# Splitting normed rows for an expert gather during the projection ahead of it

## Chip, cores and metric

The kernel runs on one core of one Trainium2 chip. The metric is device microseconds of one execution of the whole kernel; lower is better.

## The reference

One decoder layer over 512 tokens of width 1024, all in float32. The change lies where the second part, a cross-attention, ends and the third, a mixture of experts, begins:

```python
h = layer_norm(ALPHA * h + o @ w_xo, ln2_g, ln2_b)      # o: attention over 256 memory tokens
g_logits = h @ w_router_group + b_router_group           # 8 groups, the best one is taken
e_logits = h @ w_router_expert + b_router_expert         # 8 experts in it, the best two are taken
...
hb = silu(xb @ w_gate[e]) * (xb @ w_up[e])               # xb: the tokens of expert e, hidden width 256
y_rows = hb @ w_down[e]
h = layer_norm(ALPHA * h + segment_sum(y_rows * weight), ln3_g, ln3_b)
```

Each of the 64 experts has a gate, an up and a down matrix of 1 MB.

## The kernel before

The 512 tokens are four blocks (t = 0 to 3) of 128 rows, one row to a partition. The tensor `h2` holds the rows after the cross-attention.

**Output projection.** `proj_tm` (L275) computes `o @ w_xo` in two column halves. Each matrix is split into a high and a low part, since the matmul of the fast type keeps only part of a float32: `A.copy` on ScalarE (ACT) rounds to the high part, a subtraction on VectorE (DVE) or GpSimd (POOL) gives the low one. While the second half runs block by block, the loop at L1073 puts the router between its matmuls: `rows_T(t)` transposes the rows on TensorE (PE) and copies them with ACT (L959), `route(t)` makes the logits and picks experts with short DVE operations, `norm(t)` writes the normed rows (without scale and bias) on ACT, and `finish(t)` counts with PE (`prk`) which slot each token takes at its expert and writes a one-hot tile `G0[t]` on DVE (L1046, L1047).

**First gather.** After the projection, `h2_split(t)` splits the normed rows into `h2h` (ACT, L1108) and `h2l` (POOL or DVE, L1111); the two big tiles take over memory that the projection's input held (`pool2a`). `gather0(t)` multiplies them with the one-hot tile, so that the tokens of the first 256 slots are gathered, transposed, in PSUM (`px0`); `to_XT` applies the norm's scale and bias there and writes `XTs[0]`. Independently POOL applies scale and bias to `h2` itself in 32 operations of 256 columns (L1145, L1146), since the experts' results are added to it later. The two row vectors `gbc2` and `bbc2` are loaded during the projection.

**Experts.** They come in 20 columns of 128 slots, some of two and some of four or five experts. `hidden_of(c)` multiplies with the gate matrices, then with the up matrices (`pu`), and makes `hb` with a SiLU on ACT and a product on DVE (L1180). `down` transposes `hb` (`ph`), copies it to `hT` on DVE (L1251), and multiplies with the down matrices (`pd`, L1256). `scaled` splits the result into `yh` (ACT) and `yl` (DVE), and `combine` adds it to `h2` by a one-hot matmul (`pc`, L1376) and a DVE sum (L1377). Columns 0 and 1 go first. During column 0 the experts are put in order of their counts (`ppos`, `ptb`); from that DVE works out `gslot`, every token's slot (L1302). `next_pair(1)` writes the one-hot tiles `G1` from it and gathers columns 2 and 3 (`px1`, L1235, L1236). Then come the down projections of columns 0 and 1, and `ptab`, a table of weights and tokens by slot (L1332).

**What orders the work.** From the projection to `ptab`, PE, POOL and the DMA queue of SyncE (SP) run in the order in which the code is written (`manual_schedule`). DVE and ACT run in an order that a scheduler fixed when the program was built, and so does PE from column 2 on. Every engine executes its list in order.

**Weights.** `WeightStream` loads expert matrices into a ring of ten slots of 1 MB (`NSLOT`): gates and ups of column 0, then of column 1, then the downs, then column by column. A load is issued once the matmuls that read the slot before are done. Eight slots open as soon as the attention's memory is free, the last two behind the projection.

Of the kernel before, what the change touches and what calls it, by code (L numbers as in the profile page):

```python
# [60 lines left out]
def tile_layer(ctx, tc, x, mem, positions, w_in, attn_sinks, conv_w, conv_b, b_igate, b_fgate, ml_norm_g,  # L61
# [680 lines left out]
    small = ctx.enter_context(tc.tile_pool(name="small", bufs=2, reuse_waits="tile"))  # L742
    pool2a = ctx.enter_context(tc.tile_pool(name="big2a", bufs=2, reuse_waits="tile"))
    stack2b = pa.enter_context(ExitStack())
# [134 lines left out]
    stack2b.close()  # L879
    open_slots(NSLOT - 2)  # L880
    stack2c = pa.enter_context(ExitStack())
# [41 lines left out]
    rT2 = [lnw.tile([P, NK, P], name=f"rT{i}") for i in range(2)]  # L923
    gbc2, bbc2 = lnw.tile([P, D], name="gbc2"), lnw.tile([P, D], name="bbc2")

# [18 lines left out]
    slot0 = keep.tile([P, NT, 2], F32, name="slot0")  # L944
    gslot = keep.tile([P, NT, 2], F32, name="gslot")
    E = keep.tile([P, NT, 2, NE], BF16, name="E")
    Es = keep.tile([P, NT, NE], BF16, name="Es")
    scr64 = work.tile([P, 1, NE], F32, name="scr64")

    def rows_T(t):  # L950

        r = h2[:, t, :]
        rT = rT2[t % 2]
        for c in range(2):
# [59 lines left out]
    def xo_consume(b, t, ps):  # L1014
        if b == 0:
            lns2[t] = LayerNorm(small, h2[:, t, :], gbc2, bbc2, f"2{t}")
# [7 lines left out]
    for i in range(4):  # L1024
        step(gen, 4)
        if i == 2:
            nc.sync.dma_start(gbc2, row(ln2_g).to_broadcast([P, D]))
            nc.sync.dma_start(bbc2, row(ln2_b).to_broadcast([P, D]))
        wstream.ahead(i)
# [39 lines left out]
    def finish(t):  # L1069
        ranks(t)  # L1070
        onehot_tile(G0, slot0, t)

    for t in range(NT):  # L1073
        if t > 0:
            step(gen, 1)
            rows_T(t - 1)
            if t > 1:
                finish(t - 2)
            step(gen, 1)
            lns2[t - 1].scales()  # L1080
            route(t - 1)
            norm(t - 1)
        else:
            step(gen, 1)
        step(gen, 1)
    run(gen)
    stack2c.close()
    open_slots(2)
    wstream.ahead(len(wslots))
    h2h = bigtile(pool2a, "h2h", F32R).rearrange("p (t n) -> p t n", t=NT)  # L1090
    h2l = bigtile(pool2a, "h2l", F32R).rearrange("p (t n) -> p t n", t=NT)

    h2hv = h2h.rearrange("s t (k p) -> s t k p", k=NK)
    h2lv = h2l.rearrange("s t (k p) -> s t k p", k=NK)
    h2v = h2.rearrange("s t (p k) -> s t k p", k=NK)
    px0 = [(psA if c < 3 else psB).tile([P, 2, 256], F32, name=f"px0{c}", tag="psA" if c < 3 else "psB") for c in range(4)]

    def gather0(t):

        for k in range(NK):  # L1100
# [5 lines left out]
    def h2_split(t, on):  # L1106

        A.copy(h2hv[:, t], h2v[:, t])  # L1108
        n = 4 if on is V else 2
        for k in range(0, NK, n):  # L1110
            on.tensor_tensor(h2lv[:, t, k:k + n, :], h2v[:, t, k:k + n, :], h2hv[:, t, k:k + n, :].bitcast(F32), ALU.subtract)  # L1111
            yield

    rows_T(3)
    lo = h2_split(0, G)
    step(lo, 2)
    lns2[3].scales()
    run(lo)
    route(3)
    finish(2)  # L1120
    gather0(0)
    run(h2_split(1, G))
    norm(3)
    gather0(1)
    run(h2_split(2, V))
    finish(3)
    gather0(2)
    run(h2_split(3, V))
    gather0(3)
# [11 lines left out]
    for c in range(4):  # L1141
        to_XT(XTs[0], px0[c], c)
    for t in range(NT):
        for o in range(0, D, 256):
            G.tensor_tensor(h2[:, t, o:o + 256], h2[:, t, o:o + 256], gbc2[:, o:o + 256], ALU.mult)  # L1145
            G.tensor_tensor(h2[:, t, o:o + 256], h2[:, t, o:o + 256], bbc2[:, o:o + 256], ALU.add)  # L1146
    tap("h2", h2)
    for t in range(NT):
# [153 lines left out]
    V.tensor_tensor(gslot, gslot, rank, ALU.add)  # L1302
    run(next_pair(1, (psB, "psB")))
    pds01 = [list(down(hb, parts_of(c), c, f"{c}", (psB, "psB"), (psA, "psA"))) for c, hb in enumerate((hb0, hb1))]
    used[0] += COLS[0][0] + COLS[1][0]
    wstream.ahead(used[0] + len(wslots))
    gi = work.tile([P, 2, NT * 2], I32, name="gi")
    cs_ = work.tile([P, 2, NT * 2], F32, name="cs_")
# [310 lines left out]
```

## Time and profile before

| | us |
|---|---|
| three runs: median (lowest to highest) | 1273.08 (1272.89 to 1275.72) |
| the profiled execution: its own time | 1276.22 |
| its span, first to last instruction | 1274.4 |
| PE busy in the span | 1183.6 (93%) |
| DVE, ACT, POOL busy | 619.4, 372.3, 146.6 |
| moved by DMA | 268.05 MB, 210 GB/s over the span |
| mean granted TensorE clock | 0.984 of full speed |

Times in the trace count from the start of the span. A DVE or ACT time is from start to end of an instruction; a wait for a shared resource inside it counts as its time. The chain of waits follows the work that ended last back from instruction to instruction, so its pieces lie end to end. The granted clock tells at what share of its full 2.4 GHz TensorE was let run in a stretch.

### The profile page before, as it was taken

The numbers are of one execution on the slowest core, as the hardware profiler recorded it, in microseconds if no ns is written. First come the engines' busy times: TensorE is split into PE (matmuls) and PEld (weight loads), VectorE is DVE, ScalarE is ACT, GpSimd is POOL, SyncE is SP. The second block draws the span as 40 slices with busy tenths as digits, with TensorE's granted clock in tenths as the row PEclk, the third lists the DMA queues.
The fourth block names the chain that finished last, engine by engine and source line by source line (L and its number), as shares of the span: only waits on it lengthen the run. The fifth ranks groups of instructions, "written<-read, shape, count | busy, mean of one in ns | idle before, by whom it ended". The sixth has DMA issues, their size and how long they took to land.

```text
span 1274.4 us, 18547 instructions
## 1 busy us (share of the span) xinstructions
PE 1183.6 (93%) x7227; PEld 855.8 (67%) x7227; DVE 619.4 (49%) x1414; ACT 372.3 (29%) x712; POOL 146.6 (12%) x146
## 2 busy tenths in 40 slices
PE   7899999999999999999999979999999999987993
PEld 6777677777787888779888856656656556534441
DVE  5658876523244434663455785334244324313236
ACT  4334464434434322353442511101101111100201
POOL 1330000000011011231000370000000000000003
PEclk8999999999999999999999899999999999999997
DMA  6221212222223336355118138999989999998973
GB/s 184 83 67 53 65 50 67 66 68 66 77 72 90 92 98 208 103 150 165 50 67 330 67 141 347 374 420 403 382 340 386 420 412 416 419 419 359 420 285 133
DMA packets 119375, 268.05 MB, mean 210 GB/s; under 512 B 18675, under 2 KB 79091, under 8 KB 95221
## 3 DMA queue, kind: packets, MB, share of 16 engines
q1 hardware_dynamic: 118992, 265.78, 55.9%
q10 hardware_dynamic: 292, 1.06, 0.3%
q8 instruction: 58, 0.95, 0.3%
q14 instruction: 33, 0.26, 0.1%
HBM read 264.72 MB, written 2.10 MB: 209 GB/s over the span
## 4 chain that ended last, share of the span: by engine, by line
PE 73%; DVE 10%; DMA 9%; ACT 3%; issue 3%; POOL 2%; SPq 0%; ACTq 0%; POOLq 0%
PE pu L1174 11%; DMA wu<-in_w_up_dram 7%; PE pc L1376 5%; PE pd L1256 5%; PE px L1235 3%; PE px L1236 3%; PE pn L676 1%; PE pfga L246 1%; PE pfga L244 1%; PE pfgm L246 1%; PE pfqx L244 1%; PE pfga L245 1%; PE pfgm L245 1%; PE pfgm L244 1%; PE pfqx L245 1%
## 5 line engine op out<-in xcount | busy, mean ns | idle before, releaser
L238 ACT CAST wh<-wr 128x1024 fp32r<-128x1024 f32 (+1 forms) x106 | 111.1, 1049 | 258.2 <-issue 78.4
L239 DVE TENSOR_TENSOR wl<-wr,wh 128x1024 fp32r<-128x1024 f32 (+1 forms) x80 | 99.3, 1242 | 156.7 <-ACT wh L238 153.8
L239 POOL TENSOR_TENSOR wl<-wr,wh 128x1024 fp32r<-128x1024 f32 x26 | 64.6, 2485 | 447.8 <-ACT wh L238 410.9
L1174 PE MATMUL pu<-wg,arenaL 128*32 128x256 f32 (+2 forms) x1024 | 100.6, 392 | 5.8 <-issue 5.8
L1256 PE MATMUL pd<-wd,arenaR 128*32 128x512 f32 (+2 forms) x480 | 87.3, 598 | 7.5 <-DVE arenaR L1251 6.2
L1174 PE MATMUL pu<-wu,arenaL 128*32 128x256 f32 (+2 forms) x1024 | 90.0, 380 | 1.9 <-DMA wu<-in_w_up_dram 1.9
L1235 PE MATMUL px<-G,h2h 128*128 128x256 f32 x320 | 82.6, 292 | 4.6 <-DVE arenaL L1137 2.3
L1174 PEld LDWEIGHTS pu<-wg,arenaL 128*32 128x32 f32 (+2 forms) x1024 | 51.7, 123 | 43.8 <-issue 17.9
L1236 PE MATMUL px<-G,h2l 128*128 128x256 f32 x320 | 80.6, 287 | 0.0
L1376 PE MATMUL pc<-yh,oh 128*128 128x512 f32 x168 | 72.6, 433 | 1.0 <-DVE h L1377 0.5
L1174 PEld LDWEIGHTS pu<-wu,arenaL 128*32 128x32 f32 (+2 forms) x1024 | 52.0, 120 | 31.6 <-DMA wu<-in_w_up_dram 4.3
L1376 PE MATMUL pc<-yl,oh 128*128 128x512 f32 x168 | 68.2, 409 | 4.4 <-DVE yl L255 4.2
L1377 DVE TENSOR_TENSOR h<-h,pc 128x512 f32<-128x512 f32 x88 | 60.0, 685 | 24.7 <-PE pc L1376 24.2
L1235 PEld LDWEIGHTS px<-G,h2h 128*128 128x128 f32 x320 | 60.3, 189 | 16.0 <-issue 8.1
L1180 DVE TENSOR_TENSOR arenaR<-arenaR,pu 128x256 f32<-128x256 f32 x22 | 13.4, 609 | 114.9 <-ACT arenaR L1179 114.9
L1139 ACT ACTIVATE arenaL<-px,gbk 128x256 f32<-128x256 f32 x44 | 24.5, 564 | 149.9 <-PE px L1236 100.7
L255 DVE SCALAR_TENSOR_TENSOR yl<-pd,wtab,yh 128x512 fp32r<-128x512 f32 x42 | 31.2, 750 | 72.6 <-ACT yh L254 71.9
L1236 PEld LDWEIGHTS px<-G,h2l 128*128 128x128 f32 x320 | 60.3, 188 | 7.0 <-issue 6.6
L1256 PEld LDWEIGHTS pd<-wd,arenaR 128*32 128x32 f32 (+2 forms) x480 | 26.8, 120 | 51.8 <-issue 37.2
L1179 ACT ACTIVATE arenaR<-pu 128x256 f32<-128x256 f32 x22 | 8.5, 385 | 176.8 <-PE pu L1174 176.8
L96 POOL TENSOR_TENSOR rs<-ve,pow_h 128x2 f32<-128x2 f32 x2 | 1.8, 891 | 499.9 <-DVE ve L1502 499.9
L254 ACT ACTIVATE yh<-pd,wtab 128x512 fp32r<-128x512 f32 x42 | 28.5, 687 | 100.7 <-PE pd L1256 90.2
(448 smaller groups left out, 2681.4 us busy)
## 6 DMA issues: line engine op xcount, KB each, us to landing
wg<-in_w_gate_dram SPq DMA_DIRECT2D x64, 1024.0 KB, 12.8
wu<-in_w_up_dram SPq DMA_DIRECT2D x64, 1024.0 KB, 16.1
wd<-in_w_down_dram SPq DMA_DIRECT2D x60, 1024.0 KB, 11.0
wr<-in_w_in_dram SPq DMA_DIRECT2D x50, 512.0 KB, 3.6
wr<-in_w_xkv_dram SPq DMA_DIRECT2D x16, 512.0 KB, 4.1
wr<-in_w_att_branch_dram SPq DMA_DIRECT2D x8, 512.0 KB, 4.1
wr<-in_w_ml_branch_dram SPq DMA_DIRECT2D x8, 512.0 KB, 4.0
wr<-in_w_mix_out_dram SPq DMA_DIRECT2D x8, 512.0 KB, 4.7
```

What stands on the lines that cost most here:

```text
L238: A.copy(hi, raw)
L239: (G if i % 4 == 3 else V).tensor_tensor(lo, raw, hi.bitcast(F32), ALU.subtract)
L244: T.matmul(ps, lhsT=sh, rhs=mh, start=first, stop=False)
L245: T.matmul(ps, lhsT=sh, rhs=ml, start=False, stop=False)
L254: A.activation(hi, src, AF.Copy, scale=scale)
L255: V.scalar_tensor_tensor(lo, src, scale, hi.bitcast(F32), op0=ALU.mult, op1=ALU.subtract)
L1174: T.matmul(pu[sl, u * 256:(u + 1) * 256], lhsT=XT[:, k, o + sl.start:o + sl.stop], rhs=w[what][:, k, :], start=(k == 0), stop=(k == NK - 1))
L1235: T.matmul(px[:, j, :], lhsT=h2hv[:, t, 2 * c + j, :], rhs=g[:, t, :], start=(t == 0), stop=False)
L1236: T.matmul(px[:, j, :], lhsT=h2lv[:, t, 2 * c + j, :], rhs=g[:, t, :], start=False, stop=(t == NT - 1))
L1256: T.matmul(pd[sl, :], lhsT=hT[:, k, sl], rhs=w['d'][:, k, nh * 512:(nh + 1) * 512], start=(k == 0), stop=(k == 1))
L1376: T.matmul(pc, lhsT=oh[:, t * P:(t + 1) * P], rhs=y[:, ns], start=(i == 0), stop=(i == len(mms) - 1))
L1377: V.tensor_tensor(acc[:, t, ns], acc[:, t, ns], pc, ALU.add)
```

## The change

Four things move. (1) `h2h` and `h2l` get memory of their own (`poolG`), opened before the projection. The split of block t - 1 is then issued inside the projection's loop, casts on ACT, all subtractions on POOL; only block 3 is split behind it. (2) That memory is taken from the weight ring while the projection runs: three slots open early and seven late, when the projection's input and its weights are gone. (3) The scale and bias rows go into two split buffers (`wh`, `wl`) and are loaded behind the projection; POOL applies them only when `gslot` is there, held back by a copy of one of its columns to `late`. (4) The down projections of columns 0 and 1 stand before the second gather. In the first gather, half of block 0 now stands between the two transposes of block 3.

```diff
-    open_slots(NSLOT - 2)
+
+    poolG = wpools.enter_context(tc.tile_pool(name="h2p", bufs=2, side="right", reuse_waits="tile"))
+    h2h, h2l = [poolG.tile([P, NT * D], F32R, name=n, tag="big").rearrange("p (t n) -> p t n", t=NT) for n in ("h2h", "h2l")]
+    open_slots(NSLOT - 7)
...
-    gbc2, bbc2 = lnw.tile([P, D], name="gbc2"), lnw.tile([P, D], name="bbc2")
...
-    def rows_T(t):
+    def rows_T(t, cs=(0, 1)):
...
-        if i == 2:
-            nc.sync.dma_start(gbc2, row(ln2_g).to_broadcast([P, D]))
-            nc.sync.dma_start(bbc2, row(ln2_b).to_broadcast([P, D]))
         wstream.ahead(i)
...
             norm(t - 1)
+            lo = h2_split(t - 1, G)
+            step(lo, 2 if t == NT - 1 else 4)
...
     stack2c.close()
-    open_slots(2)
+    stack2a.close()
+    open_slots(7)
+    gbc2 = strm.tile([P, 1056], F32, name="gbc2", tag="wh", bufs=2)[:, :D]
+    bbc2 = strm.tile([P, 1056], F32, name="bbc2", tag="wl", bufs=2)[:, :D]
+    nc.sync.dma_start(gbc2, row(ln2_g).to_broadcast([P, D]))
+    nc.sync.dma_start(bbc2, row(ln2_b).to_broadcast([P, D]))
     wstream.ahead(len(wslots))
-    h2h = bigtile(pool2a, "h2h", F32R).rearrange("p (t n) -> p t n", t=NT)
-    h2l = bigtile(pool2a, "h2l", F32R).rearrange("p (t n) -> p t n", t=NT)
...
-    rows_T(3)
-    lo = h2_split(0, G)
-    step(lo, 2)
+    rows_T(3, (0,))
+    gather0(0, range(4))
+    rows_T(3, (1,))
     lns2[3].scales()
     run(lo)
     route(3)
+    norm(3)
     finish(2)
-    gather0(0)
-    run(h2_split(1, G))
-    norm(3)
+    gather0(0, range(4, NK))
     gather0(1)
-    run(h2_split(2, V))
+    run(h2_split(3, G))
     finish(3)
     gather0(2)
-    run(h2_split(3, V))
     gather0(3)
...
-    for t in range(NT):
-        for o in range(0, D, 256):
-            G.tensor_tensor(h2[:, t, o:o + 256], h2[:, t, o:o + 256], gbc2[:, o:o + 256], ALU.mult)
-            G.tensor_tensor(h2[:, t, o:o + 256], h2[:, t, o:o + 256], bbc2[:, o:o + 256], ALU.add)
...
     V.tensor_tensor(gslot, gslot, rank, ALU.add)
-    run(next_pair(1, (psB, "psB")))
     pds01 = [list(down(hb, parts_of(c), c, f"{c}", (psB, "psB"), (psA, "psA"))) for c, hb in enumerate((hb0, hb1))]
     used[0] += COLS[0][0] + COLS[1][0]
     wstream.ahead(used[0] + len(wslots))
+    run(next_pair(1, (psB, "psB")))
+
+    G.tensor_copy(late, gslot[:, 0, 0:1])
+    for t in range(NT):
+        for o in range(0, D, 256):
+            G.tensor_tensor(h2[:, t, o:o + 256], h2[:, t, o:o + 256], gbc2[:, o:o + 256], ALU.mult)
+            G.tensor_tensor(h2[:, t, o:o + 256], h2[:, t, o:o + 256], bbc2[:, o:o + 256], ALU.add)
```

POOL's list from the router inside the projection to the first scale and bias operations, before (`h2l` is the low part of the rows, `ln_rs` a scale of the norm, `h1` the memory of `h2`):

```order
L96 TENSOR_TENSOR ln_rs21_5894<-ln_ve21_5892,pow_h_87 128x1
L96 TENSOR_TENSOR ln_rs22_5983<-ln_ve22_5981,pow_h_87 128x1
L1111 TENSOR_TENSOR h2l_6036<-h1_3991,h2h_6035 128x256 x2
L96 TENSOR_TENSOR ln_rs23_6060<-ln_ve23_6058,pow_h_87 128x1
L1111 TENSOR_TENSOR h2l_6036<-h1_3991,h2h_6035 128x256 x6
L1145 TENSOR_TENSOR h1_3991<-h1_3991,arenaL_5523 128x256
L1146 TENSOR_TENSOR h1_3991<-h1_3991,arenaL_5523 128x256
```

The same place in the changed kernel:

```order
L1082 TENSOR_TENSOR h2l_5521<-h1_3991,h2h_5520 128x256 x4
L96 TENSOR_TENSOR ln_rs21_5893<-ln_ve21_5891,pow_h_87 128x1
L1082 TENSOR_TENSOR h2l_5521<-h1_3991,h2h_5520 128x256 x4
L96 TENSOR_TENSOR ln_rs22_5987<-ln_ve22_5985,pow_h_87 128x1
L1082 TENSOR_TENSOR h2l_5521<-h1_3991,h2h_5520 128x256 x2
L96 TENSOR_TENSOR ln_rs23_6085<-ln_ve23_6083,pow_h_87 128x1
L1082 TENSOR_TENSOR h2l_5521<-h1_3991,h2h_5520 128x256 x6
L1306 COPY late_5544<-gslot_5543 128x1
L1309 TENSOR_TENSOR h1_3991<-h1_3991,gbc2_6039 128x256
L1310 TENSOR_TENSOR h1_3991<-h1_3991,bbc2_6040 128x256
```

The subtractions of three blocks now stand between the norm's scales, inside the projection, and the copy from `gslot` stands before the scale and bias.

DVE's list before, from the slot table's last large comparison to the two copies `arenaR<-ph` that make `hT` (`pu_1` is the hidden product of column 1, `px1` a quarter of the second gather):

```order
L1330 TENSOR_TENSOR arenaR_5524<-iota_f_5525,arenaR_5524 128x1024
L1180 TENSOR_TENSOR arenaR_5524<-arenaR_5524,pu_1_6367 128x128x2
L1327 TENSOR_TENSOR arenaR_5524<-arenaR_5524 128x4x54 x2
L1329 TENSOR_TENSOR arenaR_5524<-arenaR_5524,wsel_5534 128x8x54
L1137 TENSOR_SCALAR arenaL_5523<-px10_6462,gbk_4002 128x256
L1137 TENSOR_SCALAR arenaL_5523<-px11_6481,gbk_4002 128x256
L1137 TENSOR_SCALAR arenaL_5523<-px12_6500,gbk_4002 128x256
L1251 COPY arenaR_5524<-ph_0_6538 128x256
L1137 TENSOR_SCALAR arenaL_5523<-px13_6519,gbk_4002 128x256
L1251 COPY arenaR_5524<-ph_1_6552 128x256
```

In the changed kernel, from the last two one-hot tiles of the second gather on:

```order
L1050 TENSOR_SCALAR G1_6466<-iota_f_5530,sq1_6467 128x256 x2
L1051 SCALAR_TENSOR_TENSOR G1_6466<-iota_f_5530,sq1_6467,G1_6466 128x256 x2
L1316 TENSOR_SCALAR arenaR_5529<-arenaR_5529 128x8
L1061 TENSOR_SCALAR sq3_7156<-gslot_5543 128x8
L1317 TENSOR_SCALAR arenaR_5529<-arenaR_5529 128x8
L1318 CAST arenaR_5529<-arenaR_5529 128x16
L1330 TENSOR_TENSOR arenaR_5529<-iota_f_5530,arenaR_5529 128x8x54
L1335 TENSOR_TENSOR arenaR_5529<-iota_f_5530,arenaR_5529 128x1024
L1178 TENSOR_TENSOR arenaR_5529<-arenaR_5529,pu_1_6346 128x128x2
L1249 COPY arenaR_5529<-ph_0_6430 128x256
L1332 TENSOR_TENSOR arenaR_5529<-arenaR_5529 128x4x54 x2
L1334 TENSOR_TENSOR arenaR_5529<-arenaR_5529,wsel_5539 128x8x54
```

DVE's order up to the hidden product is the same; behind it the first `hT` copy now comes at once, and the conversions of the second gather come after both copies.

## Rows read from the trace of the kernel before

**Rows 1.** Windows: stretch, its length, busy us (instructions) by engine, PEclk, DMA share, GB/s.

```profile
730.00:740.00 10.00, 5.18 (x35) 5.04 (x34) 10.00 (x18) 2.21 (x4) 9.69 (x10) 0.84 0.01 2
...
930.00:940.00 10.00, 10.00 (x98) 6.71 (x97) 6.54 (x16) 0.56 (x1) 0.00 (x0) 1.00 0.46 167
...
1100.00:1110.00 10.00, 10.00 (x47) 5.90 (x46) 5.15 (x8) 1.92 (x3) 0.00 (x0) 1.00 1.01 418
```

**Rows 2.** Chain of waits, 715 to 765 us: start, us, what.

```profile
723.93 1.97 ACT h2h L1108
...
733.37 1.27 DVE h2l L1111
...
739.00 1.00 DVE h2l L1111
...
744.14 0.36 PE px L1103
...
749.85 0.20 PE ppos L1217
...
752.32 0.21 DVE arenaR L1276
...
762.04 0.07 DVE sq L1057
```

**Rows 3.** Timeline of DVE: start, us, engine, line, operation, out<-in.

```profile
716.97 0.22 DVE L1038 CUSTOM_DVE_ANT_0 arenaR<-prk,E 128x64 f32<-128x64 f32 x1 [0.30 <-PE prk L1036]
...
717.97 0.35 DVE L1046 TENSOR_SCALAR G<-iota_f,slot 128x256 fp32r<-128x256 f32 x1
718.36 0.48 DVE L1047 SCALAR_TENSOR_TENSOR G<-iota_f,slot,G 128x256 fp32r<-128x256 f32 x1
...
731.47 0.82 DVE L1046 TENSOR_SCALAR G<-iota_f,slot 128x256 fp32r<-128x256 f32 x1
...
732.35 0.81 DVE L1047 SCALAR_TENSOR_TENSOR G<-iota_f,slot,G 128x256 fp32r<-128x256 f32 x1
...
767.18 0.62 DVE L1180 TENSOR_TENSOR arenaR<-arenaR,pu 128x256 f32<-128x256 f32 x1
```

**Rows 4.** Timeline of POOL.

```profile
730.53 0.73 POOL L1145 TENSOR_TENSOR h<-h,arenaL 128x256 f32<-128x256 f32 x1
...
738.92 1.63 POOL L1145 TENSOR_TENSOR h<-h,arenaL 128x256 f32<-128x256 f32 x1
...
758.23 0.73 POOL L1146 TENSOR_TENSOR h<-h,arenaL 128x256 f32<-128x256 f32 x1
```

**Rows 5.** Timeline of PE; in brackets the idle time before, and what ended it.

```profile
739.06 0.20 PE L1036 MATMUL prk<-Es,ustrb 128*128 128x64 bf16 x1 [4.82 <-DVE Es L991]
...
742.43 0.33 PE L1104 MATMUL px<-G,h2l 128*128 128x256 f32 x1
...
763.33 0.39 PE L1235 MATMUL px<-G,h2h 128*128 128x256 f32 x1 [0.68 <-DVE G L1047]
...
764.64 0.39 PE L1235 MATMUL px<-G,h2h 128*128 128x256 f32 x1 [0.42 <-DVE G L1047]
...
771.88 0.28 PE L1236 MATMUL px<-G,h2l 128*128 128x256 f32 x1
```

**Rows 6.** Chain of waits, 600 to 960 us, its pieces around the third hidden layer.

```profile
772.90 3.65 PE pd L1256 x16
...
781.09 1.97 PE ptab L1332 x16
783.17 4.02 PE pu L1174 x70
787.18 1.35 PE pc L1376 x5
```

**Rows 7.** Windows of 5 us under the output projection, columns as in rows 1.

```profile
685.00:690.00 5.00, 5.00 (x36) 4.55 (x34) 4.88 (x7) 1.87 (x2) 0.00 (x0) 1.00 1.01 415
...
705.00:710.00 5.00, 5.00 (x29) 4.18 (x28) 4.14 (x26) 2.09 (x4) 0.55 (x1) 1.00 0.01 3
```

More of the change, by code (lines that the diff above doesn't have):

```diff
@@ L742, in tile_layer @@
     small = ctx.enter_context(tc.tile_pool(name="small", bufs=2, reuse_waits="tile"))
-    pool2a = ctx.enter_context(tc.tile_pool(name="big2a", bufs=2, reuse_waits="tile"))
+    stack2a = pa.enter_context(ExitStack())
+    pool2a = stack2a.enter_context(tc.tile_pool(name="big2a", bufs=2, reuse_waits="tile"))
     stack2b = pa.enter_context(ExitStack())
@@ L923, in tile_layer @@
     rT2 = [lnw.tile([P, NK, P], name=f"rT{i}") for i in range(2)]
-    gbc2, bbc2 = lnw.tile([P, D], name="gbc2"), lnw.tile([P, D], name="bbc2")
+    h2hv = h2h.rearrange("s t (k p) -> s t k p", k=NK)
+    h2lv = h2l.rearrange("s t (k p) -> s t k p", k=NK)
+    h2v = h2.rearrange("s t (p k) -> s t k p", k=NK)
     csum = work.tile([P, 72], name="csum")
@@ L945, in tile_layer @@
     gslot = keep.tile([P, NT, 2], F32, name="gslot")
+    late = keep.tile([P, 1], F32, name="late")
     E = keep.tile([P, NT, 2, NE], BF16, name="E")
@@ L948, in tile_layer @@
     scr64 = work.tile([P, 1, NE], F32, name="scr64")
-    def rows_T(t):
+    def rows_T(t, cs=(0, 1)):
         r = h2[:, t, :]
         rT = rT2[t % 2]
-        for c in range(2):
+        for c in cs:
             pt = psB.tile([P, 4, P], F32, name=f"tr2{t}{c}", tag="psB")
@@ L1015, in xo_consume @@
         if b == 0:
-            lns2[t] = LayerNorm(small, h2[:, t, :], gbc2, bbc2, f"2{t}")
+            lns2[t] = LayerNorm(small, h2[:, t, :], None, None, f"2{t}")
         cs = slice(b * 512, (b + 1) * 512)
@@ L1071, in finish, with h2_split @@
         onehot_tile(G0, slot0, t)
+    def h2_split(t, on):
+        A.copy(h2hv[:, t], h2v[:, t])
+        n = 4 if on is V else 2
+        for k in range(0, NK, n):
+            on.tensor_tensor(h2lv[:, t, k:k + n, :], h2v[:, t, k:k + n, :], h2hv[:, t, k:k + n, :].bitcast(F32), ALU.subtract)
+            yield
     for t in range(NT):
@@ L1087, in tile_layer, with gather0 @@
     stack2c.close()
-    open_slots(2)
-    wstream.ahead(len(wslots))
-    h2h = bigtile(pool2a, "h2h", F32R).rearrange("p (t n) -> p t n", t=NT)
-    h2l = bigtile(pool2a, "h2l", F32R).rearrange("p (t n) -> p t n", t=NT)
[L1093 to L1100, printed above, removed]
+    stack2a.close()
[4 more added lines that the diff above has]
+    nc.sync.dma_start(bbc2, row(ln2_b).to_broadcast([P, D]))
+    wstream.ahead(len(wslots))
+    px0 = [(psA if c < 2 else psB).tile([P, 2, 256], F32, name=f"px0{c}", tag="psA" if c < 2 else "psB") for c in range(4)]
+    def gather0(t, ks=range(NK)):
+        for k in ks:
             px = px0[k // 2][:, k % 2, :]
@@ L1104, in gather0 @@
             T.matmul(px, lhsT=h2lv[:, t, k, :], rhs=G0[:, t, :], start=False, stop=(t == NT - 1 and k % 2 == 1))
[L1106 to L1112, printed above, removed]
-    rows_T(3)
-    lo = h2_split(0, G)
-    step(lo, 2)
+    rows_T(3, (0,))
+    gather0(0, range(4))
+    rows_T(3, (1,))
     lns2[3].scales()
@@ L1142, in tile_layer @@
         to_XT(XTs[0], px0[c], c)
-    for t in range(NT):
-        for o in range(0, D, 256):
-            G.tensor_tensor(h2[:, t, o:o + 256], h2[:, t, o:o + 256], gbc2[:, o:o + 256], ALU.mult)
-            G.tensor_tensor(h2[:, t, o:o + 256], h2[:, t, o:o + 256], bbc2[:, o:o + 256], ALU.add)
-    tap("h2", h2)
     for t in range(NT):
@@ L1306, in tile_layer @@
     wstream.ahead(used[0] + len(wslots))
+    run(next_pair(1, (psB, "psB")))
[4 more added lines that the diff above has]
+            G.tensor_tensor(h2[:, t, o:o + 256], h2[:, t, o:o + 256], bbc2[:, o:o + 256], ALU.add)
+    tap("h2", h2)
     gi = work.tile([P, 2, NT * 2], I32, name="gi")
```

## Prediction, made before the changed kernel was run

> **What bounds the kernel now.** I read the windows first, then the chain of waits, then the engines one by one around the place of the change. The windows show one stretch in which TensorE (PE) is starved: from 730 to 740 us it is busy 5.18 of 10 us at a granted clock of 0.84, and the DMA engines do nothing (share 0.01) [rows 1]. In the expert stage PE is busy throughout, and by 1100 us the DMA engines are full as well (1.01): the weight stream sets the pace [rows 1]. Does a gain at 740 us survive that? Between 930 and 940 us the DMA share is 0.46 [rows 1]: there every weight slot is taken and the stream waits for PE to free one. So a lead of PE at 930 us becomes a lead of the stream, and passes to the end nearly whole.
>
> The chain of waits names what starves PE. A cast of normed rows to h2h sits on ScalarE between the transposed copies of the last router block (1.97 us at 723.93). Then four subtractions to h2l sit on VectorE (DVE) between the router's short operations (1.27 us at 733.37 to 1.00 us at 739.00). The last quarter of the first gather starts at 744.14; the place table waits for the expert counts until 749.85; the slots are known at 762.04 [rows 2].
>
> **The change, step by step, from the profiled execution.** I follow two clocks: when PE ends the second hidden layer, and when the slots (gslot) are known.
>
> 1. *Casts and subtractions leave the chain.* The cast before the last router block goes: 2.0 us. The four subtractions on DVE go: about 4.2 together [rows 2]. After them, the ranks and the one-hot of the last block took from 740.00 to the matmul at 744.14, 4.1 us; the same rows took 1.9 for an earlier block (716.97 to 718.36 + 0.48) [rows 3], when GpSimd (POOL) was idle. Now POOL has ended its subtractions by then: with 0.1 to the matmul, 2.1 saved.
> 2. *What the projection pays.* The casts and most of the subtractions of blocks 0 to 2 now run under the output projection. There ScalarE is busy 2.09 and POOL 0.55 of 5 us [rows 7], so both have room. But POOL beside DVE lengthens router operations (step 3), and PE's rank matmul waits for these: at least nothing, at most two operations of 0.33 in each of two blocks, 1.3; I take 0.5. The lead at the last quarter of the gather is 2.0 + 4.2 + 2.1 - 0.5 = 7.8 us: 736.3 for 744.14.
> 3. *Counts and slots without POOL.* The scale and bias ran on POOL from 730.53 to 758.96 [rows 4], beside this chain. There a one-hot comparison took 0.82 us that takes 0.35 alone, and its second half 0.81 for 0.48 [rows 3]: 0.33 to 0.47 us extra for an operation that is hit. Between the gather and the place table that is three short ones: 1.4 us, lead 9.2. Between 752.32 and 762.04 [rows 2] it is about six at 0.4: 2.4, lead 11.6. So the second hidden layer ends at 763.33 - 0.68 - 9.2 = 753.5 [rows 5], and the slots come at 750.4.
> 4. *The new wait.* Both down projections now stand before the second gather on PE. Their first operand, hT, is a DVE copy, and ahead of it in DVE's queue are still the four one-hot tiles of the second gather, two large comparisons for the slot table and the second hidden product. That queue took from 762.04 to 767.18 + 0.62 [rows 2, 3], and with the copy 6.2 us; the gather on PE hid it. Now PE has nothing else from 753.5 on. And the scale and bias start on POOL just when the slots are known, so that some 19 DVE operations run beside them. Eight comparisons at 0.47 and 0.33 extra [rows 3] are 3.2; four of the seven tiny ones 1.4; the two large ones 0.9: 5.5 us. The bounds: nothing, if POOL always loses; and 19 times one POOL operation of 0.73 [rows 4], 13.9, if DVE always does. I take 5.5, since it comes from rows of the same operations beside the same POOL work. The copy ends at 750.4 + 6.2 + 5.5 = 762.1; PE has idled 8.6 us.
> 5. *Clock.* At 739.06 PE came out of 4.82 us of idleness, and its 16 gather matmuls ran at half speed (1.2 GHz) until 742.43, 3.4 us for 1.9 [rows 5]. After a longer idle time I expect the same at the first down projection: 0 to 3.4 us, I take 1.5.
> 6. *To the third hidden layer.* Both down projections, 772.90 to 781.09: 8.2 [rows 6]. The gather's 64 matmuls at the pace from 764.64 to 771.88 (60 of them): 7.7 [rows 5]. The slot table to the third hidden layer, 781.09 to 783.17: 2.1 [rows 6]. 762.1 + 8.2 + 1.5 + 7.7 + 2.1 = 781.6 for 783.17: **1.6 us earlier**.
> 7. *Combining.* All eight combine tiles now stand ahead of the third layer's up half. Their first use was 4.0 us behind that layer's start (787.18) [rows 6], and stays so. At most 0.5 us is lost where the third tile waits for one-hots and sums on DVE; I cost it at nothing. The added wait: gain and bias rows lie in split buffers that the second column's yh takes next, so yh on ScalarE waits for POOL's last operation. At the old pace of 0.89 (730.53 to 758.23, 31 steps) [rows 4] 32 operations end at 750.4 + 28.6 = 779.0; yh is due after 781.6. That cover of 2.6 us would be gone at a pace above 0.97, and then each us of POOL is one of PE.
> 8. *Weights.* Five gate and up tiles and two down tiles are issued when the projection ends, about 722, behind the gain and bias rows on SP's queue: 8.4 MB at 415 GB/s [rows 7] are 20 us, 2.5 us a tile. So the first up tile lands by 729 and is due at 743, the last down tile by 744 and due at 762. SP's wait for the buffers of the gain rows ends inside the projection, and only these loads are behind it. Nothing lost, nothing gained.
>
> The sum: 1276.22 - 1.6 = 1274.6 for the profiled execution. The median of the runs lies 3.1 us under it, so 1273.08 - 1.6 = **1271.5 us**. Some 0.3%, 3.8 us, is what a measurement of this kernel tells from no change. The likeliest case is thus no visible difference: a gain of some 10 us on one chain, spent on a wait that it uncovers.
>
> **Rivals.**
> *Most of the gain survives (0.36).* If the lock costs DVE's queue only half of the 5.5 us, and the clock holds, the gain is 1.6 + 2.7 + 1.5 = 5.8: 1267.3; with no loss at all 8.6: 1264.5. For it: POOL was often the one delayed, its operations went from 0.73 up to 1.63 us [rows 4]. Against it: the comparisons at 731.47 and 732.35 both lost [rows 3].
>
> *DVE loses every time (0.08).* Each of the 19 operations waits for a whole POOL operation, 13.9 for 5.5 us: the copy ends at 770.5 and the kernel is 6.8 us slower than before, 1279.9. The gain is nil from 7.1 us of loss on (0.37 for each operation); from 10.9 on the kernel is measurably slower. Against it: in no stretch of this trace did every operation lose. The Trainium skill ("SBUF — State Buffer", section "Who interferes with whom") says that DVE and GpSimd share one port pair as an exclusive lock, that whichever starts first keeps it for its whole instruction while the other fully blocks, and that DVE copies, tensor-scalar operations and operations with two SBUF inputs take part. By that rule this rival and the one before differ only in who starts first; the trace agrees so far, as both sides lose by turns [rows 3, 4].
>
> *The weights come late, or the splits don't leave the path (0.05).* If all seven tiles landed together at 744, the up half of the first hidden layer would stall 1 us, and the slots with it: 1272.5. If the projection stretches by the full 1.3 us: 1272.3.
>
> **How the numbers follow.** No visible difference holds the forecast (0.50) and the last pair of cases (0.05): 0.55. Faster by over 0.3%: 0.36. Slower by over 0.3%: 0.09, the second rival and 0.01 for what I did not see. The range reaches up to 1276.0, where the lock costs 10.0 us, and down to 1264.5, the case without any loss; outside lie most of the second rival and the tails, under 0.2. The forecast's own range, a lock of 3.3 to 7.1 us, is 1269.3 to 1273.1.
>
> **What would show it.** Right: the first down projection starts near 762 after PE has idled 6 to 10 us, its wait is for the DVE copy of hT, and the one-hot comparisons ahead of that take 0.7 to 0.8 us; the last quarter of the first gather starts near 736, the slots come near 750, the third hidden layer near 781. Step 1 is wrong if that quarter starts after 740; step 4 if PE idles under 4 us there or hT waits for something else; step 5 if the down matmuls run at full speed at once; step 8 if PE waits for a DMA before 765. The forecast falls if the third hidden layer starts before 778 or after 785, or if the lead there is not the lead at the end.

## The result, and the profile after

The changed kernel takes 1281.32 us (median of 4 runs, 1278.39 to 1283.36) against 1273.86 for the kernel before; the ratio is 1.0055, 95% interval 1.004 to 1.007. A second measurement, among the experiments, gave 1280.21 against 1274.13, ratio 1.0045 (1.0028 to 1.0061). It is 6 to 7.5 us slower, beyond the 1276.0 at which the range ended. One of the twelve executions of the kernel with the splits alone, in the table below, took 3659.21 us, for a reason that no trace here shows, and is left out of its row.

The two profiled executions show less of it: spans of 1276.6 and 1274.4 us. They have to be laid over each other first. The router's column sums (pcs) come before the work that the change moves, though its fewer early weight slots are open by then. Already there the execution of the kernel before was 2.05 us late: 687.33 against 685.28. That is within the spread of the thirteen traces that start with the change's early part, 685.28 to 689.58. So all milestones below are counted from the start of that matmul in their own trace.

The timeline of PE of the changed kernel, in brackets the idle time before and what ended it:

```profile
685.28 1.90 PE L941 MATMUL pcs<-wrt,ones 128*128 128x72 f32 x16
...
731.73 0.21 PE L1040 MATMUL prk<-Es,ustrb 128*128 128x64 bf16 x1 [3.96 <-DVE Es L998]
...
735.31 0.41 PE L1116 MATMUL px<-G,h2h 128*128 128x256 f32 x1
...
738.34 1.95 PE L1172 MATMUL pu<-wg,arenaL 128*64 128x256 f32 x16
...
753.17 0.44 PE L1247 MATMUL ph<-ident,arenaR 128*128 128x128 f32 x2
762.03 6.64 PE L1254 MATMUL pd<-wd,arenaR 128*64 128x512 f32 x16 [8.43 <-DVE arenaR L1249]
...
769.61 3.65 PE L1254 MATMUL pd<-wd,arenaR 128*64 128x512 f32 x16 [0.56 <-issue]
...
783.24 3.66 PE L1172 MATMUL pu<-wg,arenaL 128*32 128x256 f32 x64 [0.37 <-PE poe L1350]
...
804.91 1.91 PE L1254 MATMUL pd<-wd,arenaR 128*32 128x512 f32 x8
...
807.31 1.90 PE L1254 MATMUL pd<-wd,arenaR 128*32 128x512 f32 x4
...
812.54 3.62 PE L1254 MATMUL pd<-wd,arenaR 128*32 128x512 f32 x20
...
824.41 0.38 PE L1172 MATMUL pu<-wu,arenaL 128*32 128x256 f32 x1
```

The same places in the kernel before, beside [rows 5, 6]:

```profile
687.33 1.90 PE L935 MATMUL pcs<-wrt,ones 128*128 128x72 f32 x16
...
803.47 3.64 PE L1256 MATMUL pd<-wd,arenaR 128*32 128x512 f32 x32
...
819.95 0.39 PE L1174 MATMUL pu<-wu,arenaL 128*32 128x256 f32 x3
```

Three things are to be seen. The wait that was forecast is there: PE idles 8.43 us for VectorE's copy of the first down's operand, and then runs that down at 6.64 us for 3.65. The third hidden layer starts at 783.24, which is 98.0 after the column sums; before it was 95.8 (783.10 - 687.33; [rows 6] has the start of that piece of the chain at 783.17). And between the third hidden layer and the up half of the fourth column's layer, where PE has no idle time worth naming in either kernel, 36.85 us have become 41.17. The down of the third column was one piece of 32 matmuls, 3.46 us to the next work; now it is three pieces, of 1.84, 1.83 and 3.55 us.

The windows show the cost on the clock, and why the spans hide part of the loss. Of the changed kernel (columns as in rows 1):

```profile
750.00:755.00 5.00, 3.61 (x33) 2.07 (x28) 4.97 (x10) 0.38 (x1) 4.58 (x7) 1.00 1.00 413
755.00:760.00 5.00, 0.00 (x0) 0.00 (x0) 4.93 (x9) 0.00 (x0) 4.76 (x7) 0.78 1.02 424
760.00:765.00 5.00, 2.96 (x8) 1.00 (x10) 4.68 (x6) 0.00 (x0) 4.84 (x6) 0.50 0.86 359
765.00:770.00 5.00, 4.44 (x14) 1.14 (x12) 0.42 (x1) 0.00 (x0) 4.69 (x8) 0.69 0.13 23
...
1190.00:1200.00 10.00, 10.00 (x70) 5.55 (x71) 1.48 (x3) 1.70 (x3) 0.00 (x0) 1.00 1.01 419
```

Of the kernel before:

```profile
1190.00:1200.00 10.00, 10.00 (x67) 5.75 (x66) 0.60 (x1) 1.85 (x4) 0.00 (x0) 0.85 1.01 419
```

From 753.6 to 762.03 PE stands, and its granted clock goes down to 0.50, the lower of its two levels (1.2 GHz), at which the first down then mostly runs; in the kernel before the second gather filled that place. Late in the program the execution of before ran at a granted clock of 0.85 from 1190 to 1200, although PE was busy all the time, and the changed one at 1.00. Counted from the column sums, the changed execution is 5.9 us behind at the down that the kernel before starts near 1176, and 4.2 behind at the next, near 1200, and at the end: 1.7 us of the loss were made up there by chance. The second trace of the changed kernel ends 5.7 us behind. That is why the medians, and not the two spans, are the result.

### The profile page after: what moved, and what is told of

Read it like the earlier page. It is cut to its first block, busy times and chain, and to the rows that moved or that the text cites. A ratio compares the mean times of both kernels' runs of the same rounds, so it can differ in the third digit from the quotient of the medians.

```text
span 1276.6 us, 18540 instructions
## 1 busy us (share of the span) xinstructions
PE 1187.2 (93%) x7227; PEld 855.1 (67%) x7227; DVE 617.7 (48%) x1410; ACT 373.3 (29%) x712; POOL 151.9 (12%) x155
## 4 chain that ended last, share of the span: by engine, by line
PE 75%; DVE 10%; DMA 7%; ACT 3%; issue 3%; POOL 2%; SPq 0%; DVEq 0%; POOLq 0%; ACTq 0%
PE pu L1172 11%; DMA wu<-in_w_up_dram 6%; PE pd L1254 6%; PE pc L1381 5%; PE px L1233 3%; PE px L1234 3%; PE pn L676 1%; PE pp L244 1%; PE pp L245 1%; PE pp L246 1%; PE pfga L246 1%; PE pfga L244 1%; PE pfgm L246 1%; PE pfga L245 1%; PE pfgm L245 1%
## 5 line engine op out<-in xcount | busy, mean ns | idle before, releaser
L1254 PE MATMUL pd<-wd,arenaR 128*32 128x512 f32 (+2 forms) x480 | 94.0, 612 | 14.7 <-DVE arenaR L1249 13.6
L1172 PE MATMUL pu<-wg,arenaL 128*32 128x256 f32 (+2 forms) x1024 | 98.7, 392 | 6.3 <-DVE sq L1061 5.9
L1140 DVE TENSOR_SCALAR arenaL<-px,gbk 128x256 f32<-128x256 f32 x44 | 23.8, 543 | 81.6 <-ACT arenaL L1142 81.0
```

The lines of the kernel that those rows point to most:

```text
L1172: T.matmul(pu[sl, u * 256:(u + 1) * 256], lhsT=XT[:, k, o + sl.start:o + sl.stop], rhs=w[what][:, k, :], start=(k == 0), stop=(k == NK - 1))
L1254: T.matmul(pd[sl, :], lhsT=hT[:, k, sl], rhs=w['d'][:, k, nh * 512:(nh + 1) * 512], start=(k == 0), stop=(k == 1))
```

## The experiments

All milestones of the two kernels and the twelve experiments in one table: start of the column sums in the trace; start of the third column's hidden layer ("third layer") and first matmul of the up half of the fourth column's layer, counted from it; median and number of runs; ratio to the kernel before on the same chip (whose medians were 1273.86, 1274.79, 1274.13 and 1274.18 us in the four sets).

| kernel | column sums | third layer | fourth's up half | us (runs) | ratio (95%) |
|---|---|---|---|---|---|
| before | 687.33 | 95.8 | 132.6 | 1273.86 (4) | 1 |
| changed | 685.28 | 98.0 | 139.1 | 1281.32 (4) | 1.0055 (1.004 to 1.007) |
| changed, again | 689.58 | 96.7 | 137.8 | 1280.21 (6) | 1.0045 (1.0028 to 1.0061) |
| gather first | 686.57 | 90.3 | 132.5 | 1275.39 (12) | 1.0007 (0.9992 to 1.0021) |
| scale on VectorE | 685.71 | 89.1 | 130.3 | 1271.61 (12) | 0.9977 (0.9961 to 0.9993) |
| whole groups | 686.65 | 96.7 | 132.5 | 1275.64 (12) | 1.0002 (0.9989 to 1.0015) |
| these three | 686.62 | 89.9 | 128.2 | 1271.15 (12) | 0.9968 (0.9955 to 0.9981) |
| groups, PE kept busy, first try | 688.28 | 98.9 | 134.8 | 1277.37 (12) | 1.0017 (1.0002 to 1.0032) |
| groups, PE kept busy, second try | 685.55 | 95.0 | 130.8 | 1272.73 (12) | 0.9991 (0.9977 to 1.0006) |
| groups and scale on VectorE | 685.43 | 89.1 | 125.0 | 1265.37 (6) | 0.9931 (0.9914 to 0.9948) |
| three, scale in the gaps | 685.87 | 87.7 | 123.5 | 1266.13 (6) | 0.9936 (0.9914 to 0.9959) |
| scale early on POOL | 685.97 | 98.7 | 139.9 | 1281.75 (9) | 1.0053 (1.0036 to 1.007) |
| splits alone, groups | 685.56 | 95.4 | 131.4 | 1272.78 (11) | 0.9981 (0.9967 to 0.9995) |
| gather first, groups | 685.81 | 91.7 | 127.6 | 1267.33 (8) | 0.9946 (0.9926 to 0.9965) |

The fourth column's up half against 132.6 gives the time against the kernel before to within 2 us in every row. So a lead or a loss at that place reaches the end nearly whole, and each step can be priced there.

**Gather first.** The downs go back behind the second gather:

```
+    run(next_pair(1, (psB, "psB")))
     pds01 = [list(down(hb, parts_of(c), c, f"{c}", (psB, "psB"), (psA, "psA"))) for c, hb in enumerate((hb0, hb1))]
...
-    run(next_pair(1, (psB, "psB")))
```

> The changed kernel with one part undone: the second gather stands before the two down projections on TensorE again; all else stays, GpSimd's scale and bias beside it too. Wait theory (the loss is the wait for the first down's operand, 8.4 us idle, then half clock): the gather runs in that wait. It can begin when the four one-hot tiles are there (757.0 in the changed kernel), so it ends near 764; the downs need 7.7 us more, the table 2.1: the third hidden layer starts at 774 (772 to 776) instead of 783.2, and the time is 8 to 12 us under the changed kernel's 1281, so 1269 to 1273. Split theory (the loss is that the third column's down matmuls no longer stand in whole groups of four, 7.2 us for 3.5, as the order of this kernel shows again): the third hidden layer may start early, but the four us between it and the fourth stay. If the split is all of the loss, the time stays over 1277.

The wait theory had the direction: the third layer came 6.4 to 7.7 us earlier, and PE idled 1.90 us at most. The size was too hopeful: the gather ended at 765.3, not 764, the layer started at 776.83, since POOL still runs beside VectorE's queue, and the time fell by 4.8 to 5.9 us, not by 8 to 12. The split theory had its part too: 42.2 us from the third layer to the fourth's up half. Both losses are real.

**Scale on VectorE.** POOL's 32 operations become eight of VectorE, behind the second down's operand:

```
-            G.tensor_tensor(h2[:, t, o:o + 256], h2[:, t, o:o + 256], gbc2[:, o:o + 256], ALU.mult)
-            G.tensor_tensor(h2[:, t, o:o + 256], h2[:, t, o:o + 256], bbc2[:, o:o + 256], ALU.add)
...
+    V.tensor_scalar(late, hTs[1][:, 0, 0:1], 0.0, 1.0, op0=ALU.mult, op1=ALU.add)
+    for t in range(NT):
+        V.scalar_tensor_tensor(h2[:, t, :], h2[:, t, :], late, gbc2, op0=ALU.mult, op1=ALU.mult)
+        V.tensor_tensor(h2[:, t, :], h2[:, t, :], bbc2, ALU.add)
```

> The changed kernel with the scale and bias taken from GpSimd: VectorE does them in eight operations of 1024 columns, held back until the second column's down operand is copied. GpSimd is silent from 732 us on; the TensorE order is that of the changed kernel. Lock theory (VectorE's queue ahead of the first down takes 11.6 us beside GpSimd, 6.2 alone): the one-hot comparisons fall from 0.82 to 0.31 and 0.9 to 0.44 us each, the first down starts at 756.6 instead of 762.0 after 3.2 us idle instead of 8.4; the third hidden layer at 775 to 778; time 5 to 8 us under the changed kernel's 1281, 1273 to 1276, so level with the kernel before. Rival (queue length, not the lock, makes the wait): the first down still starts after 760 and the time stays over 1278.

The groups of VectorE's operations from 750 to 762 us (mean ns behind the busy time). Changed kernel:

```profile
L1051 DVE SCALAR_TENSOR_TENSOR G<-iota_f,sq,G 128x256 fp32r<-128x256 f32 x4 | 3.6, 945 | 0.0
L1050 DVE TENSOR_SCALAR G<-iota_f,sq 128x256 fp32r<-128x256 f32 x4 | 3.2, 850 | 0.0
L1335 DVE TENSOR_TENSOR arenaR<-iota_f,arenaR 128x1024 f32<-128x1024 f32 x1 | 1.7, 1739 | 0.0
```

With POOL silent:

```profile
L1051 DVE SCALAR_TENSOR_TENSOR G<-iota_f,sq,G 128x256 fp32r<-128x256 f32 x4 | 1.7, 477 | 0.0
...
L1328 DVE TENSOR_TENSOR arenaR<-iota_f,arenaR 128x1024 f32<-128x1024 f32 x1 | 1.2, 1218 | 0.0
L1050 DVE TENSOR_SCALAR G<-iota_f,sq 128x256 fp32r<-128x256 f32 x4 | 1.2, 345 | 0.0
```

VectorE's last step to the slots and its copy for the first down, changed kernel:

```profile
749.95 0.17 DVE L1300 TENSOR_TENSOR gslot<-gslot,rank 128x8 f32<-128x8 f32 x1
...
761.57 0.41 DVE L1249 COPY arenaR<-ph 128x256 f32<-128x256 f32 x1
```

With POOL silent:

```profile
750.39 0.17 DVE L1300 TENSOR_TENSOR gslot<-gslot,rank 128x8 f32<-128x8 f32 x1
...
756.15 0.41 DVE L1249 COPY arenaR<-ph 128x256 f32<-128x256 f32 x1
```

And PE there:

```profile
756.63 3.65 PE L1254 MATMUL pd<-wd,arenaR 128*64 128x512 f32 x16 [2.58 <-DVE arenaR L1249]
```

Same operations, same order on PE: the comparisons cost 850 and 945 ns beside POOL, 345 and 477 alone. From the slots to the end of the copy it is 6.0 us (750.56 to 756.56) for 11.9 (750.12 to 761.98): POOL's work beside that queue, the lock of the expectation, takes 5.9 us. With 2.58 us of idleness in place of 8.43 the down also runs at full speed. The third layer comes 7.5 to 8.8 us earlier, the time falls by 8.6 to 9.7 us, more than the 5 to 8 expected. The lock theory holds, and its rival falls.

**Whole groups.** The third column's PE work is kept in the order in which it is written:

```
+        if c == 2:
+            whole = ctx.enter_context(ExitStack())
+            whole.enter_context(tc.manual_schedule(engines={mybir.EngineType.PE}))
         hb = hidden_of(c, (psU, "psU"), {})
...
         ys.append(outputs_of(c, hb))
+        if c == 2:
+            whole.close()
```

> The changed kernel with the TensorE order of the third column (hidden layer, combining of the first two, its down) fixed as written, so that all its up and down matmuls stand in groups of four; nothing before 783 us changes. Split theory: the down of that column falls from 7.2 to 3.5 us, its up half from 5.2 to 4.1, and the fourth column's up half starts near 820 instead of 824.6; since half of a delay there came through to the end (4.5 at 825, 2.2 at the end), the time falls by 2 to 4.5 us, to 1277 to 1279. Wait theory alone: nothing changes, over 1280.

The timeline of PE of this kernel:

```profile
762.46 6.34 PE L1254 MATMUL pd<-wd,arenaR 128*64 128x512 f32 x16 [8.43 <-DVE arenaR L1249]
...
783.30 3.66 PE L1172 MATMUL pu<-wg,arenaL 128*32 128x256 f32 x64 [0.37 <-PE poe L1350]
786.75 3.66 PE L1172 MATMUL pu<-wu,arenaL 128*32 128x256 f32 x64
...
803.06 3.64 PE L1254 MATMUL pd<-wd,arenaR 128*32 128x512 f32 x32
```

The wait at 762 is untouched and the down is one piece again. The fourth's up half comes at 132.5 for 137.8 to 139.1, and the time falls by 4.6 to 5.7 us, more than expected, since the loss reaches the end whole. From the third layer to the fourth's up half it is now 35.88 us, 1.0 less than in the kernel before (36.85), whose own order has smaller splits. The down has four experts, with the matrices wd20 to wd23. In the split order those of its first column half stood apart: wd20 and wd21, three gather matmuls, wd22, 27 gather matmuls, then wd23 with the whole second half. Each matmul uses 32 columns of the array, for each expert a quarter (a tile) of its own. In a whole group they pass at 0.11 us each (3.46 / 32); the eight of wd20 and wd21 took 0.23 each (1.84 / 8), the four of wd22 alone 0.46 each (1.83 / 4). The up half of the same column lost 1.1 us against the kernel before in the same way. The Trainium skill ("TensorEngine Tiling (Array Packing)", section "Key Properties") says that different tiles of the array can execute in parallel; that agrees with the row of 32, and the split rows show that the neighbours in PE's order must be of different tiles for it.

**These three together.**

> All three together: gather before downs, scale and bias on VectorE behind the downs' operands, whole groups in the third column. If the three losses are what they seem and add up: the gather starts within 1 us of the second hidden layer's end (753.5), ends at 761, the third hidden layer starts at 770 to 772 (783.2 in the kernel before), the fourth column's up half near 808 instead of 820; the lead of 12 us passes to the end with 6 to 12: 1262 to 1268. If leads are lost downstream in the full weight stream, it ends at 1270 or above though the third hidden layer starts early.

Only in part: the ratio of 0.9968 is below 1, but 1271.2 us misses the 1262 to 1268. A new wait had come in, and it was the repair's own. The timeline of PE of this kernel:

```profile
772.01 0.27 PE L1348 MATMUL poe<-ident,arenaR 128*1 128x128 f32 x1
776.49 6.13 PE L1172 MATMUL pu<-wg,arenaL 128*32 128x256 f32 x64 [4.20 <-issue]
```

And that of VectorE:

```profile
773.79 2.35 DVE L1332 TENSOR_TENSOR h<-h,bbc 128x1024 f32<-128x1024 f32 x2
776.06 0.21 DVE L1338 TENSOR_SCALAR wtab<-ptab 128x54 f32<-128x54 f32 x1
```

VectorE's scaling now ran in one piece of 9.3 us ahead of its read of the slot table, and PE's third layer, which starts when the table is read, stood 4.20 us and came back at the lower clock (6.13 us for 3.66).

**The changed kernel again**, unaltered, because its four runs and its trace disagreed.

> The changed kernel itself, unaltered, once more: its first measurement had four runs, and its profiled execution (1278.4) was the lowest of them. If those four were fair: median 1279 to 1282, ratio to the kernel before 1.004 to 1.007. If they were drawn from executions in which TensorE's clock happened to fall more often: 1276 to 1278.5, ratio 1.001 to 1.003, as the lead of the trace (2.2 us later at the end of the span) says.

The first of the two readings holds: 1280.21, with 8.43 us of idleness and 6.36 us for the first down in this trace too.

**PE kept busy**, to price the clock alone: whole groups, and 64 matmuls that nobody reads in the 8.4 us of idleness. First try, ahead of the transposes (`phw` is the whole PSUM tile, half of which they fill):

```
...
+        if tag == "0":
+            for k in range(64):
+                T.matmul(phw[:, 256:512], lhsT=h2hv[:, 0, 0, :], rhs=G0[:, 0, :], start=True, stop=True)
         for k in range(2):
             T.transpose(ph[:, k, :], hb[:, k, :], ident)
```

> The kernel with whole groups, and 64 matmuls of 128x256 whose results nobody reads, put on TensorE between the second hidden layer and the transposes for the first down (7.6 us by the gather's pace of 0.118, of the 8.4 us in which it idled). Their outputs go to unused columns; the rest is computed as before. Clock theory (the first down took 6.64 us for 3.65 because TensorE came out of idleness at the lower clock): the first down takes 3.7 us, the third hidden layer starts at 780.3 instead of 783.3, the fourth column's up half near 816.4 instead of 819.3, and the time is 2 to 3 us under that kernel's 1275.6. Rival (the lower clock comes anyway, a little later, or the lead is lost downstream): same as that kernel within 1 us.

Neither: it was 1.7 us slower. The scheduler put VectorE's copy behind three further operations, so the first down started 3.3 us later (79.1 for 75.8), after 3.26 us of idleness. That is no test of the clock. Second try, the same matmuls behind the transposes, into unused columns of another PSUM tile:

```
             T.transpose(ph[:, k, :], hb[:, k, :], ident)
+        if tag == "0":
+            for k in range(64):
+                T.matmul(pcn[:, 256:512], lhsT=h2hv[:, 0, 0, :], rhs=G0[:, 0, :], start=True, stop=True)
```

> The kernel with whole groups again, with 64 unread matmuls of 128x256 (7.6 us), this time behind the transposes for the first down, so that VectorE's order stays that of the kernel without them (in the first try VectorE's copy of the operand was put 3.3 us later). Counted from the start of the router's column sums, 686.7 in the kernel with whole groups: there the first down starts at 75.8 and the third hidden layer at 96.7. Clock theory: the first down still starts at 75.8 to 76.2, takes 3.7 us instead of about 6.5, the third hidden layer comes at 93.7 to 94.2; time 2 to 3 us under the 1275.6 of the kernel with whole groups. Rival (the clock falls anyway, or the lead is lost): within 1 us of it.

The timeline of PE of the second try:

```profile
753.56 7.84 PE L1250 MATMUL pcn<-G,h2h 128*128 128x256 f32 x64
762.36 3.65 PE L1257 MATMUL pd<-wd,arenaR 128*64 128x512 f32 x16 [0.96 <-DVE arenaR L1252]
```

The first down waits for the same copy and takes 3.65 us. From its start to the third layer it is 18.1 us for 20.8, and the median is 2.9 us under that of whole groups. The two were measured on different chips, though: against the kernel before beside each, the ratios 0.9991 and 1.0002 are 1.4 us apart, and their intervals overlap. So by the traces 2.7 us of the change's loss are the clock, after this one stretch of idleness; in the time that is not clear of noise. The third layer itself came at 95.0, a little later than expected, because this execution reached the first hidden layer 0.9 us later.

**Groups and scale on VectorE**, the downs still first.

> Whole groups, and scale and bias on VectorE, with the downs still ahead of the gather: the two repairs of the losses without undoing the order of downs and gather. If the two are additive: third hidden layer at 775 as with the scale on VectorE alone, fourth column's up half 4.3 us earlier than there, 811.5 (816.0 there, 814.8 with all three), time 1267 to 1269.5, under the 1271.2 of all three, whose third hidden layer was held at 776.5 by VectorE's scaling ahead of its read of the table. If the stream of weights eats the lead: 1271 or above.

The two repairs add up: 89.1 and 125.0, and 1265.37 us, below the expected span. This is the fastest that was run: 0.5 to 0.9% under the kernel before.

**All three, with the scaling in VectorE's gaps** (one block behind the last one-hot of the first gather, the others behind the table's comparison and behind the first down's copy).

> All three, with VectorE's eight scaling operations spread over its idle stretches (one block while the last quarter of the first gather runs, the rest between the second gather's copies and between the two down operands), so that the table is read at once. The third hidden layer starts at 772.5 to 773.5 (776.5 with all of them in one piece, 783.1 in the kernel before), the fourth column's up half at 808 to 810; since 6.6 us of lead at the third layer became 5.4 at the end with all three, 10 us should become 8: time 1265 to 1268. If the first block's scaling delays the first gather's copies: 1 us later throughout.

As expected at the third layer (87.7) and in time (1266.13); not to be told from the run before by the times.

**Scale early on POOL**: the change without its holding back, `late` taken out and the loop put ahead of `route_weights`, as in the kernel before.

> The changed kernel with one part undone: GpSimd's scale and bias are not held back until the slots are known but follow the last subtraction, from about 732, as in the kernel before; TensorE's order stays. Lock theory: the 32 operations now meet the count and slot chain (one-hots, counts, the twelve or so operations before the slots) and end near 760: the slots come 3 to 5 us later than in the changed kernel (750.4), the one-hots behind them still meet GpSimd's last third, and the first down starts at 760 to 764 (762.0). The time is within 3 us of the changed kernel's 1280, since the loss only moves from one stretch of VectorE's queue to another. Rival (holding back is what costs): the first down starts at 757 and the time falls to 1275.

POOL's last operation of the 32, in this kernel's timeline:

```profile
756.93 0.74 POOL L1148 TENSOR_TENSOR h<-h,bbc 128x256 f32<-128x256 f32 x1
```

VectorE's last step to the slots, and its copy for the first down:

```profile
757.11 0.58 DVE L1304 TENSOR_TENSOR gslot<-gslot,rank 128x8 f32<-128x8 f32 x1
...
763.29 0.41 DVE L1253 COPY arenaR<-ph 128x256 f32<-128x256 f32 x1
```

The lock theory's picture, though with another split than expected: POOL ends at 757.67 and the slots at 757.69, 7 us later than in the changed kernel. The queue behind them then runs alone, 6.0 us to the end of the copy. The first down starts at 763.76, and the time is the same. POOL's 25.5 us of work cost VectorE's chain 6 to 7 us wherever in that chain they lie.

**Splits alone**: gather first, scale early on POOL, whole groups; what is left of the change are the splits in the projection with their memory, the later loads of the two rows and the order within the first gather.

> What the change is named for, alone: the splits in the projection and their own memory; gather before downs and scale and bias early on GpSimd as in the kernel before, third column in whole groups. If the splits in the projection really shorten the chain: counted from the router's column sums, the first hidden layer starts at 53 (59.0 in the kernel before), the slots 3 to 5 us later than in the changed kernel, the third hidden layer at 90 to 92 (95.8 before), the fourth column's up half at 126 to 128 (132.7): time 1268 to 1271, 4 to 6 us under the kernel before. If GpSimd's work beside the counts takes it all back: 1273 to 1276.

The first hidden layer starts at 53.4 for 59.0, and the third at 95.4 for 95.8. PE at the second gather, and the window behind it (columns as in rows 1):

```profile
758.59 0.58 PE L1237 MATMUL px<-G,h2h 128*128 128x256 f32 x1 [3.28 <-DVE G L1050]
```

```profile
760.00:765.00 5.00, 5.00 (x24) 5.00 (x25) 4.54 (x12) 0.56 (x1) 0.00 (x0) 0.50 1.01 423
```

The second expectation was met in the time. Of the 5.6 us, 2.6 go where PE waits for the one-hots of the second gather (3.28 us idle, 0.68 before), which wait for slots that POOL has delayed; 2.2 more go behind it, since PE came back at a granted clock of 0.50 and the gather took 10.9 us for 8.7. At the end 1.4 us of gain remain, and of the 1.2 at the fourth's up half 0.9 come from the whole groups (35.98 us from the third layer, for 36.85): what the change is named for is worth 0.4 us here, with POOL's scaling early.

**Gather first, whole groups**, scale held back on POOL as in the change.

> Gather before downs and whole groups, scale and bias held back on GpSimd as in the change. Counted from the router's column sums: third hidden layer at 90.3 as with the gather first alone, fourth column's up half at 126.5 to 127.5 (132.5 there, 128.2 with VectorE scaling in one piece): time 1269 to 1271, some 5 us under the gather first alone (1275.4). If the split of the groups was not worth 5 us there: over 1273.

The third layer came at 91.7, 1.4 later than expected; the fourth's up half at 127.6 is above the expected span by 0.1, and 1267.33 us is below the expected span. Against the splits alone only the holding back differs, and here it is worth some 5 us (5.5 by the medians, 4.5 by the ratios); with the downs first it was worth nothing. The waits of PE show the cover:

```profile
766.91 3.65 PE L1254 MATMUL pd<-wd,arenaR 128*64 128x512 f32 x16 [0.52 <-DVE arenaR L1249]
```

The first down waits 0.52 us for its copy, where it waited 8.43 with the downs first: VectorE's long queue behind the slots hides under the gather on PE.

## Why the prediction was wrong

The forecast was 1.6 us faster at the third hidden layer, passed to the end. Measured: 2.2 later there (0.9 in the second trace), and 6.5 later (5.2) one column on. The 3.8 us missing at the third layer are mainly the lead (1.8) and the clock at the first down (1.5); the 4.3 behind it are step 7. By its steps:

*Steps 1 to 3, the lead.* Right but for the clock. VectorE had the last one-hot ready 8.1 us earlier (at 733.85 for 743.99, each counted from its column sums), where 7.8 were worked out for the quarter that it starts:

```profile
733.37 0.48 DVE L1051 SCALAR_TENSOR_TENSOR G<-iota_f,slot,G 128x256 fp32r<-128x256 f32 x1
```

But the last quarter of the first gather came only 6.8 us earlier (50.0 after the column sums for 56.8), and the first hidden layer 5.9. PE had come out of 3.96 us of idleness at 731.73, and the last two quarters ran mostly at the lower clock, 0.21 us a matmul. So the slots came 9.8 earlier for 11.6, the end of the second hidden layer 7.4 for 9.2 (8.4 in the second trace, where the clock fell later). Step 1 counted the lead and not the clock behind it.

*Step 4, the new wait.* Right in kind and size. PE idled 8.43 us for 8.6; it waited for VectorE's copy of hT; the lock took 5.9 us for 5.5. That the copy ended at 761.98, for 762.1, is luck: this execution was 2.05 us early at the column sums, and counted from there the copy came 1.9 us later than worked out, 1.8 of them the lead that the slots lacked. The rule of the Trainium skill ("SBUF — State Buffer", section "Who interferes with whom") agrees with the comparisons at 345 ns alone and 850 beside POOL. That POOL's operations beside them are the cause is shown by the run without them; that it is a lock is the page's reading, which no run here tells from another way of sharing. They lose about 0.5 us each, less than a whole POOL operation, so the rival in which VectorE loses every time at full price did not happen; that its 1279.9 us lies near the measured time is a coincidence.

*Step 5, the clock.* Mis-sized: 1.5 taken from bounds of 0 to 3.4; it was 3.0 and 2.7 in the two traces, and keeping PE busy gave 2.7 back in the trace and 1.4 to 2.9 in the time.

*Step 6, the durations.* The gather took 7.65 us for 7.7; the downs 11.2 for 9.7, by the clock.

*Step 7, combining.* **This step failed.** "At most 0.5 us is lost ...; I cost it at nothing." The wait that this sentence prices did not come: from 783.20 to 824.40 PE was busy 41.16 of 41.20 us. The order of PE that the scheduler made behind the slot table was read for the place of the combine tiles and for their first use alone. It had also pulled the third column's down apart, and with it the overlap of four narrow matmuls: 3.8 us in the down and 1.1 in the up half; the rest gave a little back, so it is 4.3 in all. The sum had no term for it, and no rival either. What the runs showed in its place: with whole groups and nothing else the changed kernel is level with the one before (1.0002): no visible difference, as was forecast for the change as a whole. Its 1275.64 us is within the forecast's range, but by luck in part: the third layer is 0.9 us late there, not 1.6 early, and whole groups make the stretch behind it 1.0 us shorter than before. The wait for POOL in that step was not touched: POOL ended at 776.55, the first yh began at 783.06.

*Step 8, the weights.* Right: PE waited for no DMA before 765.

*The lead at the third layer is the lead at the end.* Wrong by step 7: 2.2 us of loss there were 6.5 a column later. From the fourth's up half on it holds, to within 2 us in every row of the table. Why the scheduler split the groups was not tried.

## What to carry to other kernels

Before leading a chain earlier, ask which queue its end comes to meet and what covered that queue: here holding work back was worth some 5 us under the gather's cover and nothing without it. Read the order of an engine behind the change as closely as at the change: narrow matmuls that run four abreast lose that as soon as other work stands between them. And lay two traces over each other at a place ahead of the work that the change moves, before any difference of a few us is read from them.

## What was not expected of the hardware

POOL's 32 operations of 0.73 us cost VectorE's chain 6 to 7 us at either place, and eight VectorE operations of about 1.2 us do the same work in 9.7: the engine that seemed free was the dear one. Narrow matmuls of 128x512 took 0.11 us each in whole groups of four tiles, 0.23 in pairs and 0.46 standing alone. And the granted clock fell, in some executions, in stretches in which PE was busy throughout, as from 1190 to 1200 (0.85 with 10.00 of 10 us busy); in 35 executions of the kernel before, the three shortest (1271.84 to 1272.37 us) had a mean granted clock of 0.985 to 0.987, the three longest (1278.96 to 1279.87) 0.978 or 0.979.
